# Attention heads of a streaming encoder: sample steps moved into the next head, a third gate tile, bf16 masks, cached values loaded at another place

## The chip, the cores and the metric

The kernel runs on one core of one Trainium2 chip. The metric is the time of one execution on the device in microseconds (us), as the median over runs. TensorE is called PE, its weight load PEld; VectorE is DVE, ScalarE ACT, GpSimd POOL. SP is the engine that issues most DMA transfers, in a queue that is worked off in order.

## The reference

One step of an encoder with two layers: a recurrent layer, then a stick-breaking attention layer with 16 heads of 128. There is one prompt of 512 frames and there are 8 samples of 16 frames, each with 512 cached frames of keys and values. Cut to the attention:

```
def sb_block(q, q_pos, k, v):
    z = einsum('bqhd,bshd->bhqs', q, k) * (HEAD_DIM ** -0.5)
    mask = arange(k.shape[1])[None, :] < q_pos[:, None]
    log_keep = where(mask, log_sigmoid(-z), 0.0)
    log_after = cumsum(log_keep, axis=3, reverse=True) - log_keep
    attn = where(mask, exp(log_sigmoid(z) + log_after), 0.0)
    return einsum('bhqs,bshd->bqhd', attn, v)

def stick_breaking_mixer(hn, k_all, v_all, w_in, w_out):
    q, zg = split(hn @ w_in, 2, axis=-1)
    o = stick_breaking(q.reshape(B, T, N_HEADS, HEAD_DIM), k_all, v_all)
    return (o.reshape(B, T, D_ATT) * silu(zg)) @ w_out
```

The rest of the layer (norms, modulation, residual) and the recurrent layer lie outside the change.

## The kernel before

All 640 frames (512 of the prompt, 128 of the samples) stay on the chip in columns, split into a high and a low part, and each product is three matmuls (high by high, low by high, high by low: the lines L108, L109 and L110 of a helper). The attention layer is done head by head, in `heads`. While head h is attended to, TensorE also works out the query and the gate of head h+1, by a scheme of block products with fewer multiplications. These are 180 matmuls of 320 columns a head, into banks named `psh`; they are cut into 8 pieces, one for each `q` in the order below (a generator that is asked for its next piece). The gate of a head lies in the tile `z`, and the attention's result is multiplied into it.

The steps of one head, by the letters of the order:

- P, the prompt's scores: 9 matmuls of `kh` and `ql`, `kl` and so on into three banks z3, z2, z1 (L1702 to L1704), and the scores against the samples' new keys `kn` (L1809). Behind each bank `sticks` follows, on ACT: Abs, Exp, Ln (L1637, L1638, L1639); on DVE: max and add (L1642), the scan with `keep` (L1645), a subtraction (L1648); on ACT the closing exponential (L1649); and on POOL the multiply by `mask` (L1653).
- S0, S1, the samples' scores against the cached keys `ck`, four samples each, into `zc` (L1727), with sticks of their own.
- V0, V1, the turns of the prompt's weights: transposes into `pa` (L1713), 7 in V0 and 3 in V1, evacuated by ACT into `ath` and by DVE into `atl` (L1720).
- T0, T1, the turns of the samples' weights: four transposes into `pas` (L1751), which ACT evacuates to `at`, and one into `pan` (L1755), which DVE evacuates to `an`. At its start T issues the loads of two tiles of cached values `cv` (512 KB each, two slots in all).
- M0, M1, the samples' sums `pos`: 4 matmuls with the new values `vn` (L1763), 16 with `cv` (L1768), then ACT evacuates to `ob` (L1771).
- C0, C1, the close: a transpose of `ob` into `pot` (L1775), which DVE multiplies into the gate `z` (L1778). C1 also splits the finished head (`oh` on ACT, L1790, and the rest on DVE, L1791) and writes both to DRAM from POOL's queue.
- O, the prompt's sum `po` (12 matmuls), multiplied into the gate by DVE.
- L and U load the next head's keys and values, K and W split them, N loads the next head's first cached keys.

The last head has an order of its own, in which `q` is a piece of the output product with `w_out_b` (`acc`), and Z the last gates; behind its scores the queue of SP loads the finished heads back (`yh`, `yl`, 20 transfers) and then the output's weights (`wr`).

The two lines that set the order are

```
    LAST = "P S0 q q q S1 V0 q V1 q Z T0 M0 O q C0 q T1 q M1 q C1 q"
    ORDER = "P q q S0 L q q V0 V1 S1 T0 O U q M0 q T1 N K q C0 M1 W q C1"
```

A scheduler then orders the instructions of each engine by readiness and priority; splits of weights (L1367, L1368, L1379) and evacuations of query products (L1530, L1535) have a raised priority.

Of the kernel before, what the change touches and what calls it, by code (L numbers as in the profile page):

```python
# [11 lines left out]
F32 = mybir.dt.float32  # L12
# [38 lines left out]
class Trunk:  # L51
# [1238 lines left out]
    def attention_consts(self, ap):  # L1290


        G = self.nc.gpsimd
        self.mask = [ap.tile([P, n], F32, name=f"mask{i}") for i, n in enumerate((P, TS))]
        self.keep = [ap.tile([P, n], F32, name=f"keep{i}") for i, n in enumerate((PAST, PAST + TS))]
        for v in self.mask + self.keep:
            G.memset(v, 1.0)

        def before(v, base):

            G.affine_select(v, v, pattern=[[-1, v.shape[1]]], compare_op=ALU.is_gt, fill=0.0, base=-base, channel_multiplier=1)

        before(self.mask[0], 0)
        before(self.keep[0], 1 - (PAST - P))
        for j in range(4):
            r = slice(32 * j, 32 * j + 32)
            before(self.mask[1][r, :], 0)
            before(self.keep[1][r, :], 1 - PAST)
# [155 lines left out]
    def query_tiles(self, ap):  # L1464
# [3 lines left out]
        z = ap.tile([P, T], F32, tag="z", name="z", bufs=2)  # L1468
# [219 lines left out]
    def attention(self, h, ap, qkv, zs):  # L1688
# [56 lines left out]

        def sample_turn(g):
            e = st[f"es{g}"]
            st["cv"] = [cached_values(4 * g + 2 * u) for u in range(2)]
# [10 lines left out]
        def sample_out(g):  # L1759
# [4 lines left out]
            if g == 0:  # L1764
                st["vn"] = new_values(1)
            for i in range(4):
                for j in range(4):
                    mm(po[32 * j : 32 * j + 32, 0:P], at[:, i, 32 * j : 32 * j + 32], cvs[j // 2][:, 4 * (j % 2) + i, :],  # L1768
                       start=False, stop=i == 3, **kw)
            ob = st["ob"] = ap.tile([P, P], F32, tag="ob", name="ob", bufs=1)  # L1770
# [61 lines left out]
        st = {"vn": new_values(0)}  # L1832
        steps = {"P": prompt_scores, "O": prompt_out}
# [10 lines left out]
    LAST = "P S0 q q q S1 V0 q V1 q Z T0 M0 O q C0 q T1 q M1 q C1 q"  # L1844
    ORDER = "P q q S0 L q q V0 V1 S1 T0 O U q M0 q T1 N K q C0 M1 W q C1"

    def heads(self, count=NHEAD):
        with self.pool("att") as ap:
# [9 lines left out]
            k, v = self.keys_split(ap, keys), self.values_split(ap, values)  # L1858
            for h in range(count):
# [4 lines left out]
                for step in (self.ORDER if more else self.LAST).split():  # L1864
# [5 lines left out]
                    elif step in steps:  # L1870
                        steps[step]()
                    elif more and step == "L":
# [7 lines left out]
                    elif more:  # L1880
                        v = self.values_split(ap, values)
        return out
# [136 lines left out]
```

## Time and profile before

| | us |
|---|---|
| median of 3 runs | 2858.66 |
| lowest, highest | 2856.97, 2867.83 |
| profiled execution: span | 2852.1 |
| profiled execution: its own total | not listed |
| heads 0 to 15 in the span | 2005.92 to 2648.68 |
| head 0 | 45.95 |
| heads 1 to 14, together | 550.77 |
| head 15 | 46.04 |

The span runs from the first to the last instruction of the profiled execution; the runs' times hold what lies around it as well, so the median stands 6.6 above the span. A head is counted from its first score matmul (L1702, 512 columns) to that of the next; head 15 runs to the end of the stage. In the rows quoted below, a wait row names the waiting engine, tile and line, what ended the wait, the sum of the waits in us, their count and the longest; a timeline row has the start in us, the duration in us, engine, line, operation, out<-in, tile sizes and count, and in brackets the idle time before it.

### The profile page before, as it was taken

The numbers are of one execution on the slowest core, as the hardware profiler recorded it, in microseconds if no ns is written. First come the engines' busy times: TensorE is split into PE (matmuls) and PEld (weight loads), VectorE is DVE, ScalarE is ACT, GpSimd is POOL, SyncE is SP. The second block draws the span as 40 slices with busy tenths as digits, with TensorE's granted clock in tenths as the row PEclk, the third lists the DMA queues.
The fourth block names the chain that finished last, engine by engine and source line by source line (L and its number), as shares of the span: only waits on it lengthen the run. The fifth ranks groups of instructions, "written<-read, shape, count | busy, mean of one in ns | idle before, by whom it ended". The sixth has DMA issues, their size and how long they took to land.

```text
span 2852.1 us, 48054 instructions
## 1 busy us (share of the span) xinstructions
PE 2785.0 (98%) x18340; PEld 2459.3 (86%) x18340; DVE 2034.8 (71%) x3344; ACT 1666.2 (58%) x2846; POOL 439.1 (15%) x732
## 2 busy tenths in 40 slices
PE   6999999999999999999999999999999999999998
PEld 4799999999999987777787899867888889887887
DVE  7678777777777766766866866667877877776335
ACT  5576556655665556665655555553666766666223
POOL 0012212221222111112220000122101111111000
PEclk9999999999999999999999999999999999999999
DMA  9966766676766666676776233575466666668636
GB/s 339 331 145 157 166 161 153 158 164 160 161 149 164 141 228 209 206 251 190 238 255 218 92 117 109 183 267 192 145 205 189 194 197 191 199 199 287 188 111 229
DMA packets 249094, 544.49 MB, mean 191 GB/s; under 512 B 23496, under 2 KB 108616, under 8 KB 247712
## 3 DMA queue, kind: packets, MB, share of 16 engines
q1 hardware_dynamic: 201616, 377.05, 41.2%
q0 software_dynamic: 47248, 164.38, 23.2%
q8 instruction: 144, 2.36, 0.3%
q14 instruction: 86, 0.70, 0.1%
HBM read 499.97 MB, written 41.37 MB: 190 GB/s over the span
## 4 chain that ended last, share of the span: by engine, by line
PE 80%; DVE 4%; ACT 4%; DMA 3%; issue 2%; POOL 0%; SPq 0%; DVEq 0%; POOLq 0%; ACTq 0%
PE acc L108 7%; PE acc L110 7%; PE acc L109 7%; PE pa L108 4%; PE pa L110 4%; PE pa L109 4%; PE psh L108 3%; PE psh L110 3%; PE psh L109 3%; PE pc L110 3%; PE pc L109 3%; PE pc L108 3%; PE acck L108 3%; PE acck L109 2%; PE acck L110 2%
## 5 line engine op out<-in xcount | busy, mean ns | idle before, releaser
L108 PE MATMUL acc<-wh,yh 128*128 128x512 f32 x940 | 371.0, 395 | 0.5 <-ACT wh L93 0.4
L110 PE MATMUL acc<-wh,yl 128*128 128x512 f32 x940 | 365.5, 390 | 1.3 <-DVE yl L962 1.3
L109 PE MATMUL acc<-wl,yh 128*128 128x512 f32 x940 | 366.4, 390 | 0.1
L94 DVE TENSOR_TENSOR wl<-wr,wh 128x1024 fp32r<-128x1024 f32 x151 | 186.5, 1238 | 217.0 <-ACT wh L93 216.6
L93 ACT ACTIVATE wh<-wr 128x1024 fp32r<-128x1024 f32 x151 | 159.6, 1057 | 267.7 <-PE acc L110 220.7
L108 PEld LDWEIGHTS acc<-wh,yh 128*128 128x128 f32 x940 | 176.7, 188 | 54.0 <-issue 15.7
L110 PEld LDWEIGHTS acc<-wh,yl 128*128 128x128 f32 x940 | 176.3, 188 | 38.8 <-DVE yl L962 1.7
L109 PEld LDWEIGHTS acc<-wl,yh 128*128 128x128 f32 x940 | 176.5, 188 | 36.3 <-DVE wl L94 0.7
L193 DVE TENSOR_TENSOR wa<-wa 128x1024 f32<-128x1024 f32 (+1 forms) x160 | 191.5, 1247 | 11.8 <-ACT wa L192 11.2
L110 PE MATMUL pa<-xs,wl 128*128 128x320 f32 x630 | 194.8, 309 | 0.5 <-DVE wl L94 0.5
L108 PE MATMUL pa<-xs,wh 128*128 128x320 f32 x630 | 194.7, 309 | 0.0
L109 PE MATMUL pa<-xs,wh 128*128 128x320 f32 x630 | 194.7, 309 | 0.0
L93 ACT ACTIVATE wh<-sum 128x896 fp32r<-128x896 f32 x102 | 96.9, 950 | 143.0 <-PE pa L109 46.5
L192 ACT ACTIVATE wa<-wa 128x1024 bf16<-128x1024 f32 x160 | 159.3, 1046 | 25.5 <-DVE wa L193 12.0
L546 POOL DMA_DIRECT2D sum<-w_in_a_dram x90 | 79.1, 882 | 490.5 <-DVE wl L94 208.8
L108 PE MATMUL psh<-nh,wl 128*128 128x320 f32 x480 | 150.8, 314 | 2.1 <-DVE z L1535 2.1
L110 PE MATMUL psh<-nh,wl 128*128 128x320 f32 x480 | 150.1, 313 | 0.0
L109 PE MATMUL psh<-nl,wl 128*128 128x320 f32 x480 | 149.4, 311 | 0.0
L93 ACT ACTIVATE wh<-rv 128x256 fp32r<-128x256 f32 (+1 forms) x108 | 51.8, 480 | 145.8 <-PE pa L109 95.2
L108 PE MATMUL acck<-wh,nh 128*128 128x512 f32 x320 | 127.8, 401 | 5.7 <-DVE keep L1263 3.5
L110 PE MATMUL pc<-xs,wl 128*128 128x320 f32 x420 | 129.9, 309 | 0.7 <-DVE wl L94 0.7
L108 PE MATMUL pc<-xs,wh 128*128 128x320 f32 x420 | 130.0, 310 | 0.0
(489 smaller groups left out, 8595.9 us busy)
## 6 DMA issues: line engine op xcount, KB each, us to landing
wa<-w_ada_dram POOLq DMA_DIRECT2D x120, 512.0 KB, 5.2
wr<-w_out_a_dram SPq DMA_DIRECT2D x96, 512.0 KB, 4.5
sum<-w_in_a_dram POOLq DMA_DIRECT2D x90, 448.0 KB, 5.7
wa<-w_ada_dram SPq DMA_DIRECT2D x72, 512.0 KB, 6.4
wr<-w_in_b_dram SPq DMA_DIRECT2D x64, 512.0 KB, 4.3
ck<-cache_k_dram SPq DMA_DIRECT2D x64, 512.0 KB, 5.2
cv<-cache_v_dram SPq DMA_DIRECT2D x64, 512.0 KB, 5.7
wr<-w_out_b_dram SPq DMA_DIRECT2D x55, 512.0 KB, 4.2
```

Source lines behind the costliest of these rows:

```text
L93: self.split_at = nc.scalar.activation(hi[:, :n], raw, AF.Copy).ins
L94: nc.vector.tensor_tensor(lo[:, :n], raw, hi[:, :n].bitcast(F32), ALU.subtract)
L108: mm(out, sh, mh, start=start, stop=False, **kw)
L109: mm(out, sh, ml, start=False, stop=False, **kw)
L110: return mm(out, sl, mh, start=False, stop=stop, **kw)
L192: nc.scalar.activation(parts[i], raw, AF.Copy)
L193: nc.vector.tensor_tensor(parts[2] if i else raw, raw, parts[i], ALU.subtract)
L546: self.nc.gpsimd.dma_start(self.big[tag], self.quarter(w, i), accum_op=ALU.add)
```

## The change

M1 and C1 of a head are left out of its own order and run inside the next head, as `m1` and `c1`: the second sum behind the prompt's scores, the close after one piece of query products. X stands behind m1 and loads the new values and the first two tiles of cached values; the second two are issued behind M0's matmuls, so that each load stands right behind the last sum that uses its slots. The turns V0, V1 and T0 are set apart by pieces of products, T0 stands ahead of S1, M0 ahead of O. The last head's order takes m1, X and c1 in the same way. The gate `z` gets a third tile, since the gate of the head before is now in use longer; masks and keeps are bf16, which takes 2368 bytes a partition less (the third z takes 2560).

```diff
@@ -1291,8 +1291,8 @@
 
 
         G = self.nc.gpsimd
-        self.mask = [ap.tile([P, n], F32, name=f"mask{i}") for i, n in enumerate((P, TS))]
-        self.keep = [ap.tile([P, n], F32, name=f"keep{i}") for i, n in enumerate((PAST, PAST + TS))]
+        self.mask = [ap.tile([P, n], BF16, name=f"mask{i}") for i, n in enumerate((P, TS))]
+        self.keep = [ap.tile([P, n], BF16, name=f"keep{i}") for i, n in enumerate((PAST, PAST + TS))]
         for v in self.mask + self.keep:
             G.memset(v, 1.0)
 
@@ -1465,7 +1465,7 @@
         qh = ap.tile([P, TP], F32R, tag="qh", name="qh", bufs=1)
         ql = ap.tile([P, TP], F32R, tag="ql", name="ql", bufs=1)
         qs = ap.tile([P, P + TS], F32, tag="qs", name="qs", bufs=1)
-        z = ap.tile([P, T], F32, tag="z", name="z", bufs=2)
+        z = ap.tile([P, T], F32, tag="z", name="z", bufs=3)
         self.q = (qh, ql, qs, z)
         return self.q
 
@@ -1743,9 +1743,12 @@
             dma(c, I["cache_v"][b0 : b0 + 2, :, h, :].rearrange("b (i p) d -> p (b i) d", p=P))
             return c
 
+        def values_begin(g):
+            st["vn"] = new_values(g)
+            st["cv"] = [cached_values(4 * g + 2 * u) for u in range(2)]
+
         def sample_turn(g):
             e = st[f"es{g}"]
-            st["cv"] = [cached_values(4 * g + 2 * u) for u in range(2)]
             ps = one("pas")
             for i in range(4):
                 tr(ps[:, P * i : P * i + P], e[:, P * i : P * i + P], self.ident)
@@ -1761,12 +1764,12 @@
             po = one("pos")
             for j in range(4):
                 mm(po[32 * j : 32 * j + 32, 0:P], an[:, 32 * j : 32 * j + 32], st["vn"][:, j, :], start=True, stop=False, **kw)
-            if g == 0:
-                st["vn"] = new_values(1)
             for i in range(4):
                 for j in range(4):
                     mm(po[32 * j : 32 * j + 32, 0:P], at[:, i, 32 * j : 32 * j + 32], cvs[j // 2][:, 4 * (j % 2) + i, :],
                        start=False, stop=i == 3, **kw)
+            if g == 0:
+                values_begin(1)
             ob = st["ob"] = ap.tile([P, P], F32, tag="ob", name="ob", bufs=1)
             A.activation(ob, po[:, 0:P], AF.Copy)
 
@@ -1829,8 +1832,8 @@
         o = zs
         if h == NHEAD - 1:
             o = self.outs.tile([P, 2, 3 * HALF], F32R, tag="ks1", name="o", bufs=1)[:, 0, :T].bitcast(F32)
-        st = {"vn": new_values(0)}
-        steps = {"P": prompt_scores, "O": prompt_out}
+        st = {}
+        steps = {"P": prompt_scores, "O": prompt_out, "X": lambda: values_begin(0)}
         for g in range(2):
             steps[f"V{g}"] = lambda g=g: prompt_turn(g)
             steps[f"T{g}"] = lambda g=g: sample_turn(g)
@@ -1841,8 +1844,8 @@
 
 
     STAY = (NHEAD - 2,)
-    LAST = "P S0 q q q S1 V0 q V1 q Z T0 M0 O q C0 q T1 q M1 q C1 q"
-    ORDER = "P q q S0 L q q V0 V1 S1 T0 O U q M0 q T1 N K q C0 M1 W q C1"
+    LAST = "P m1 X S0 q c1 q q S1 V0 q V1 q Z T0 M0 O q C0 q T1 q M1 q C1 q"
+    ORDER = "P m1 X q c1 q S0 L q V0 q V1 T0 q S1 M0 N O U q C0 K q W T1 q"
 
     def heads(self, count=NHEAD):
         with self.pool("att") as ap:
@@ -1856,6 +1859,7 @@
             keys, values = self.keys_load(0, ap), self.values_load(0, ap)
             self.ck = self.cached_keys(0, 0, ap)
             k, v = self.keys_split(ap, keys), self.values_split(ap, values)
+            before = {}
             for h in range(count):
                 qh, ql, qs, zs = self.q
                 steps = self.attention(h, ap, (qh, ql, qs, *k, *v), zs)
@@ -1869,6 +1873,8 @@
                             self.silu(ap, zs, j)
                     elif step in steps:
                         steps[step]()
+                    elif step in ("m1", "c1"):
+                        before.get(step.upper(), lambda: None)()
                     elif more and step == "L":
                         keys = self.keys_load(h + 1, ap)
                     elif more and step == "U":
@@ -1879,6 +1885,7 @@
                         k = self.keys_split(ap, keys)
                     elif more:
                         v = self.values_split(ap, values)
+                before = steps
         return out
```

On TensorE, where one head ends and the next begins (head 6; `pot` is a close, `pos` a sum, `z` with a number a bank of scores, of which only the first and the last are shown). Before:

```order
L1775 MATMUL pot<-ident,ob 128x128
L1763 MATMUL pos<-vn,an 32x128 x4
L1768 MATMUL pos<-cv,at 32x128 x16
L108 MATMUL psh<-nh,wh 128x320
...
L1775 MATMUL pot<-ident,ob 128x128
L1702 MATMUL z_23239<-kh,qh 128x512
...
L1809 MATMUL z_23270<-kn,qs 32x16 x8
L108 MATMUL psh<-nh,wh 128x320
```

After:

```order
L1702 MATMUL z_23206<-kh,qh 128x512
...
L1812 MATMUL z_23237<-kn,qs 32x16 x8
L1766 MATMUL pos<-vn,an 32x128 x4
L1769 MATMUL pos<-cv,at 32x128 x16
L108 MATMUL psh<-nh,wh 128x320
...
L1778 MATMUL pot<-ident,ob 128x128
L108 MATMUL psh<-nh,wl 128x320
```

Before, the second sum stood between the close C0 and 12 products, and C1 ended the head. Now it stands behind the scores, 27 products lie between it and its close, and 33 behind that; a head ends with 12 products behind the turn T1.

On TensorE in the middle of the same head, the turns and the sums. Before:

```order
L1713 MATMUL pa<-ident,e 128x128 x7
L1727 MATMUL zc<-ck,qs 32x512 x4
...
L1713 MATMUL pa<-ident,e 128x128
...
L1713 MATMUL pa<-ident,e 128x128 x2
...
L1751 MATMUL pas<-ident,e 128x128 x4
...
L1755 MATMUL pan<-ident,e 16x128
L109 MATMUL psh<-nl,wl 128x320
L108 MATMUL po<-ath,vh 128x512
...
L1763 MATMUL pos<-vn,an 32x128 x4
L1768 MATMUL pos<-cv,at 32x128 x16
```

After:

```order
L1713 MATMUL pa<-ident,e 128x128 x7
...
L1713 MATMUL pa<-ident,e 128x128 x3
...
L1754 MATMUL pas<-ident,e 128x128 x4
L1758 MATMUL pan<-ident,e 16x128
...
L1727 MATMUL zc<-ck,qs 32x512 x4
L1766 MATMUL pos<-vn,an 32x128 x4
L1769 MATMUL pos<-cv,at 32x128 x16
L108 MATMUL po<-ath,vh 128x512
```

Before, S1 and three gaps of 5 products, then one of 4 and one of 1, lay between the turns and the prompt's sum. Now 24 products lie between V0 and V1, 10 between V1 and T0, `pan` stands directly behind `pas`, and S1 and M0 stand behind T0 and 2 products, ahead of the prompt's sum.

On ACT behind the start of a head, after the change (`ez` belongs to the gate, `e` to the sticks; z_23206 is z3, z_23219 z2, z_23237 z1):

```order
L1637 ACTIVATE e<-z_23206 128x512
L1458 ACTIVATE ez<-ez 128x320
L1638 ACTIVATE e<-e 128x512
...
L1638 ACTIVATE e<-e 128x256
L1530 ACTIVATE qr<-psh 128x320
L1367 ACTIVATE wh<-wr 128x512
L1649 ACTIVATE e<-e 128x512
L1639 ACTIVATE e<-e 128x256
L1774 ACTIVATE ob<-pos 128x128
```

Before, `ob` of the second sum stood ahead of all of these, in the head it belonged to:

```order
L1448 ACTIVATE qs<-qr 128x128
L1771 ACTIVATE ob<-pos 128x128
L1367 ACTIVATE wh<-wr 128x512
L1457 ACTIVATE ez<-z 128x320
L1790 ACTIVATE oh<-z 128x640
```

The evacuation of the second sum moved behind the closing exponential of z3, and one weight split (L1367) stands between the first Abs and that exponential where there were two.

On SP's queue in the last head. Before:

```order
L949 DMA yh<-odh 128x640
L1743 DMA cv<-cache_v_dram 128x8x128 x2
L103 DMA wr<-w_out_b_dram 128x1024 x3
L1743 DMA cv<-cache_v_dram 128x8x128 x2
L103 DMA wr<-w_out_b_dram 128x1024 x7
```

After, from the head's start:

```order
L949 DMA yh<-odh 128x640
L1738 DMA vn<-out_v_dram 16x4x128
L1743 DMA cv<-cache_v_dram 128x8x128 x2
L1684 DMA ck<-cache_k_dram 128x2x512 x2
L949 DMA yl<-odl 128x640
...
L1743 DMA cv<-cache_v_dram 128x8x128 x2
L103 DMA wr<-w_out_b_dram 128x1024 x7
```

The first two tiles moved ahead of the transfers of finished heads; the second two moved from behind three pieces of `w_out_b` to ahead of all of them.

## The prediction

> **What bounds the kernel now.** I read the page's first part, then the stage the change touches cut into windows, then PE's waits there, then the timeline of one head.
>
> ```profile
> span 2852.1 us, 48054 instructions
> PE 2785.0 (98%) x18340; PEld 2459.3 (86%) x18340; DVE 2034.8 (71%) x3344; ACT 1666.2 (58%) x2846; POOL 439.1 (15%) x732
> ...
> 2005.92:2051.87 45.95, 41.67 (x320) 35.24 (x318) 41.38 (x82) 33.41 (x78) 4.51 (x8) 1.00 0.48 146
> 2051.87:2602.64 550.77, 545.99 (x4755) 487.68 (x4754) 424.56 (x800) 372.47 (x829) 67.05 (x140) 1.00 0.64 197
> 2602.64:2648.68 46.04, 39.81 (x266) 29.49 (x265) 26.75 (x44) 25.89 (x48) 4.55 (x7) 0.93 0.95 330
> ...
> 2631.00:2637.00 6.00, 4.43 (x41) 3.11 (x37) 1.46 (x3) 2.28 (x3) 0.00 (x0) 0.52 0.89 317
> ```
>
> The window rows (stretch, length, busy PE, PEld, DVE, ACT, POOL, granted clock, DMA share, GB/s) are head 0, heads 1 to 14, head 15, and a piece of head 15. A head runs from its first prompt score to the next head's. TensorE is the bound: in heads 1 to 14, 39.34 us each, it is busy for 99%. [...]
>
> ```profile
> PE pa L1713 <- DVE atl L1720: 3.0, 4, 0.9
> PEld pan L1755 <- issue: 4.2, 12, 0.5
> PEld po L108 <- ACT at L1753: 2.3, 12, 0.2
> PE psh L108 <- DVE z L1535: 2.1, 1, 2.1
> PE zc L1727 <- issue: 1.0, 1, 1.0
> PE pos L1763 <- DMA vn<-out_v_dram: 0.5, 1, 0.5
> PE pos L1768 <- DMA cv<-cache_v_dram: 5.2, 2, 4.0
> ```
>
> These are waits (who, for whom: sum, count, longest): three rows of heads 1 to 14, three of head 0, one of head 15. No wait in the middle heads is large; the large one is the last head's, for cached values.
>
> Starts and durations of single matmuls, head 6 and, for the last four rows, head 13:
>
> ```profile
> 2250.16 0.48 PE L1702 MATMUL z<-kh,qh 128*128 128x512 f32 x1
> 2252.48 0.41 PE L108 MATMUL psh<-nh,wh 128*128 128x320 f32 x1
> ...
> 2269.61 0.93 PE L1713 MATMUL pa<-ident,e 128*128 128x128 f32 x7
> 2270.46 1.06 PE L1727 MATMUL zc<-ck,qs 128*32 128x512 f32 x8
> 2271.46 0.42 PE L108 MATMUL psh<-ks,wh 128*128 128x320 f32 x1
> 2271.71 0.31 PE L109 MATMUL psh<-ks,wh 128*128 128x320 f32 x1
> ...
> 2275.10 0.30 PE L108 MATMUL psh<-nh,wl 128*128 128x320 f32 x1
> 2275.55 0.27 PE L1755 MATMUL pan<-ident,e 128*16 128x128 f32 x1
> 2275.57 0.39 PE L109 MATMUL psh<-nl,wl 128*128 128x320 f32 x1
> 2275.94 0.50 PE L108 MATMUL po<-ath,vh 128*128 128x512 f32 x1
> 2276.27 0.40 PE L109 MATMUL po<-atl,vh 128*128 128x512 f32 x1
> 2276.51 0.39 PE L110 MATMUL po<-ath,vl 128*128 128x512 f32 x1
> 2276.74 0.33 PE L108 MATMUL po<-ath,vh 128*128 128x384 f32 x1
> ...
> 2560.05 0.27 PE L1775 MATMUL pot<-ident,ob 128*128 128x128 f32 x1
> 2560.25 0.42 PE L1763 MATMUL pos<-vn,an 16*32 16x128 f32 x8
> 2560.60 1.08 PE L1768 MATMUL pos<-cv,at 128*32 128x128 f32 x32
> 2561.61 0.42 PE L108 MATMUL psh<-nh,wh 128*128 128x320 f32 x1
> ```
>
> And a stretch of head 6 in which TensorE does nothing but query products (psh; length, PE busy, clock, DMA):
>
> ```profile
> 2253.00:2261.30 8.30, 8.30 (x59) 1.00 0.42 139
> ```
>
> Each lasts 0.4, so two or three of the 59 began before the stretch: they start 0.147 us apart. Prompt sums of 512 columns (po) settle at 0.23 (2276.51 to 2276.74). Beside that, starts at a change of kind show its price: 0.25 from the first psh after scores to the second, 0.20 from pot to pos, only 0.02 from a transpose to psh.
>
> **The change part by part.** The matmuls stay the same in number and shape; what moves is which stand next to which.
>
> *Waits that go, heads 1 to 14.* Before, the second prompt turn V1 follows V0 at once and waits for the evacuation of its bank: 3.0 us in four waits, from the row. Now 24 products (3.5 us) lie between: 0. The transpose pan stood behind one psh and started 0.45 after it, against 0.147 in a run: 0.30. Now it follows the pas transposes directly, and T0 stands ahead of S1 and the sum: 0.30 x 14 = 4.2, which is also the wait row's sum. Before, po followed one psh and waited a little on ACT: 0.37 to its start and 0.33 to the second product against 0.23, 0.14 + 0.10 = 0.24, x 14 = 3.4. Now M0 stands between. Together -10.6.
>
> *Switching.* A head now has 9 stretches of psh where it had 10. One less saves its entry and slow first product, (0.23 - 0.147) + (0.25 - 0.147) = 0.19. The old pot to pos step (0.20) becomes pot to psh (0.02): -0.18. The old pa to zc step, also about 0.2 (the last of 7 transposes starts near 2270.27, zc at 2270.46), becomes pa to psh: -0.17. Against this stand z to pos and pos to po, which no row shows; bounds are 0 (0.02, transpose to psh) and 0.20 (pot to pos); I take 0.1 each, the middle, since neither row is nearer. And zc to pos: by the row of zc to psh it is no dearer than before. Sum -0.54 + 0.2 = -0.34 a head, x 14 = -4.8. Ends: 0 (both steps full, the pa step not gained) and -7.6 (both free).
>
> *Waits that come.* Placing the second sum behind the prompt's scores puts its evacuation `ob` on ACT's queue behind the closing exponential of the prompt's first sticks, and C1's transpose waits for `ob`. Here is what ACT does there before:
>
> ```profile
> 2252.28 0.58 ACT L1637 ACTIVATE e<-z 128x512 f32<-128x512 f32 x1
> 2252.76 0.46 ACT L1459 ACTIVATE ez<-ez 128x320 f32<-128x320 f32 x1
> 2253.12 0.62 ACT L1638 ACTIVATE e<-e 128x512 f32<-128x512 f32 x1
> ...
> 2258.37 0.64 ACT L1649 ACTIVATE e<-e 128x512 f32<-128x512 f32 x1 [0.27 <-DVE e L1648]
> ```
>
> PE reaches C1's transpose at 2.32 (scores, 2250.16 to 2252.48) + 1.36 (M1: 0.35 for vn, 1.01 for cv) + 27 x 0.147 + 0.1 = 7.8 us after the head's start. On ACT the order lists 16 steps from the first Abs to `ob`: eight of 512 columns at 0.5, four of 320 at 0.36 (both by the starts above), three of 256 at about 0.27, `ob` 0.2: 6.45. The Abs stood 2.12 into the head, behind the gate's copy `oh` (640 columns, about 0.6), which now stands behind `ob`, so I put it at 1.4: `ob` ready at 7.85. That is even with PE's 7.8, so I take 0.1 a head, and 0.1 more for the first sample sum M0, which follows T0's evacuation `at` by S1 (1.0 us) alone. Sum +0.2 x 14 = +2.8. Ends: 0, if both are in time; +21, if the closing exponential stays at 8.2 as before: then `ob` is ready 0.5 + 0.3 + 0.3 later, at 9.3, 1.5 behind PE, x 14. I stay near the lower end because before two weight splits of 512 columns (L1367) stood between the first Abs and that exponential and one does now, and on DVE one of two such operations between the scan and L1648 went too. Queued behind the waiting transpose is all of PE.
>
> *Head 0.* No M1 and C1 stand at its end, 1.36 + 0.3 less; each head passes them on, and they come back in head 15, where PE waits for DMA in any case. The vn wait (0.5) goes, as vn is loaded at its head's start. The scores' second part stands earlier, with the key split put ahead on DVE, which takes most of the 1.0 of the zc wait, while the 2.1 for DVE at L1535 stays. Sum -3; ends -6 (that too, and the next evacuations follow) and 0 (the split delays the others).
>
> *Last head.* Before, SP put both loads of cached values for M0 behind 20 transfers of gated rows (yl, yh):
>
> ```profile
> 2622.77 1.96 SPq L1743 DMA_DIRECT2D cv<-cache_v_dram  x2
> ...
> 2630.73 0.64 PE L1768 MATMUL pos<-cv,at 128*32 128x128 f32 x4 [4.04 <-DMA cv<-cache_v_dram]
> ...
> 2633.76 1.06 ACT L93 ACTIVATE wh<-wr 128x1024 fp32r<-128x1024 f32 x1 [7.27 <-DMA wr<-w_out_b_dram]
> 2634.06 1.01 SPq L1743 DMA_DIRECT2D cv<-cache_v_dram  x2
> ```
>
> Now M0's values go ahead of them, and the wait of 5.2 and the slow matmuls behind it (clock 0.52 in 2631 to 2637: 4.43 busy, so about 2.1 over full speed) go: -7.3. What is late next is the same queue. The DMA engines are busy for 0.95 of this head (330 GB/s), and ACT waits 7.27 us for the first piece of w_out_b, so the output's products can't start before 2633.8 however early M0 is. This piece now stands behind 1 MB more, 3.2 us at 330 GB/s, since M1's values (two of 512 KB) keep the place M0's had. M1 also waits for those. PE has only prompt sums and two small sums to do meanwhile. So I take 0: the wait changes its name. Ends: -7.3 (all of it gained) and +3.2.
>
> On that slow clock, the Trainium skill's page "TensorE: Matmul & The Clock Gate", section "Part 1: The HAM clock gate (the "warmup" mystery)", states that the clock is halved after an idle window of about 3.4 us. The granted 0.52 right behind a wait of 4.04 us agrees. By it, a last head that waits in pieces shorter than that would keep its full clock, which is the 2.1 us in the -7.3 end; by my term of 0, it waits once more as long and loses it again.
>
> *No cost.* Masks in bf16 and the third z tile: the multiplies by mask run on POOL, which is busy for 67.05 of 550.77 us, and PE's wait at pa is on DVE's, not POOL's work; the scans that read keep run on DVE (424.56 of 550.77 us), over the same number of elements, so a slower scan would find slack. The third z tile takes away a reuse that has no row in PE's waits: 0. Of the loads issued behind the last sum that uses their two slots, the cached values have the longest way:
>
> ```profile
> cv<-cache_v_dram SPq DMA_DIRECT2D x64, 512.0 KB, 5.7
> ```
>
> They are needed 10 us after issue or later by the order (over 60 products and the turns between), which covers 5.7. With that cover gone each of 28 sums could wait up to 5.7.
>
> *Sum.* -10.6 - 4.8 + 2.8 - 3 + 0 = -15.6: span 2852.1 to 2836.5. The profiled execution's own total is not shown; the median of the runs, 2858.66, is 6.6 above the span, and 2836.5 + 6.6 = 2843.1. A change counts as one from about 0.5% (14.3 us: below 2844.4 or above 2873.0), so this forecast lies just past it.
>
> **The rivals.**
> - *New small waits eat half the gain.* Everything removed is 0.2 to 0.3 us a piece, and a wait of 0.4 a head at `ob`, M0 or the pas bank costs 5.6. For it: `ob` and PE are even in my count, ACT was late by 0.27 at the very exponential. Against it: PE's waits before are small throughout. 2843.1 + 8 (0.4 and a little more in 14 heads, and at head 0) = about 2851.
> - *C1 waits for `ob`* (slower). The closing exponential stays at 8.2: +21 instead of +2.8 gives -15.6 + 18.2 = +2.6, 2861.3; with the switching at its poor end 2866. It turns the change into a loss from 1.3 us of wait a head (18.4/14), and slower by 0.5% from 2.3 ((18.4 + 14.3)/14). For it: DVE was the releaser of that exponential and keeps most of its load. Against it: fewer steps stand ahead on both engines.
> - *The last head's wait really vanishes.* If the flood and w_out_b have slack that I don't see: -15.6 - 7.3 = -22.9, 2835.8. Against it: the 7.27 us wait of ACT on the same queue.
> - *The order does nothing*: PE's 99% means that what it saves at one boundary it loses at the next. Only if the 0.30 at pan and the 0.24 at po are PE's draining, and are paid at pas or S1 instead: then only the switching, head 0 and the pa wait stay, 2848 to 2856.
>
> **How the numbers follow.** The forecast (2838 to 2848) gets 0.50, small new waits 0.25, the vanishing last wait 0.10, no effect 0.05, waiting for `ob` 0.10. Faster by over 0.5% are the forecast's part under 2844.4, about 0.35, the last-head case 0.10, and 0.04 of the small waits, where they hit less than I set: 0.49. Slower by over 0.5% are the `ob` case from 2.3 us a head, 0.04, and sums that wait for their values in every head as well, 0.03: 0.07. Within: 0.44. The range goes from 2829.9 (the last-head case with switching at its better end and head 0 too: -22.9 - 2.8 - 3 = -28.7) to 2861 (the `ob` case as worked out); outside are a longer `ob` wait or waits for values, about 0.1, and some 0.05 below.
>
> **What would show it.** In the changed profile, heads 1 to 14 should take about 38.4 us each (39.34 - 12.6/14), head 15 again some 46, and the rows of pa, pan and po should be gone from PE's waits. A row of pot waiting on ACT `ob` of 0.5 us or more a head means the `ob` rival; pos waiting on DMA cv in the middle heads, that the loads moved too late. In the last head I expect pos to wait for cv still, now M1's, or acc for wh. I am wrong if PE's starts around pan and po keep 0.3 gaps elsewhere, or if the last head gets shorter by over 4 us.

## The result and the profile after

The changed kernel is slower: 2885.68 us median (2882.40 to 2889.36, 5 runs) against 2860.08 for the kernel before (2856.97 to 2867.83, 5 runs). The ratio is 1.0090, with a 95% interval of 1.0079 to 1.0102. The forecast was 2843.1 with a range of 2829.9 to 2861.0, 15.6 us faster; the change costs 25.6 us. The profiled execution after the change has a time of 2885.68 us and a span of 2883.8, so what lies around the span is about 2 us. If that holds before as well, most of the 6.6 us between the median and the span there comes from a profiled execution that was faster than the median. The forecast, a difference added to that median, isn't touched by this.

The page's first lines after the change, and windows for head 0, heads 1 to 14, and head 15 to the end (columns as in the prediction):

```profile
span 2883.8 us, 48097 instructions
PE 2790.6 (97%) x18340; PEld 2459.7 (85%) x18340; DVE 2037.1 (71%) x3344; ACT 1664.9 (58%) x2846; POOL 443.0 (15%) x732
...
2008.95:2053.48 44.53, 39.83 (x306) 34.54 (x305) 40.67 (x80) 33.36 (x78) 4.19 (x8) 1.00 0.49 151
2053.48:2631.43 577.95, 546.63 (x4727) 484.54 (x4725) 426.61 (x803) 370.16 (x829) 69.89 (x140) 1.00 0.59 188
2631.43:2883.84 252.41, 236.78 (x1159) 191.29 (x1159) 111.89 (x147) 87.03 (x136) 12.51 (x21) 0.97 0.62 198
```

Heads 1 to 14 take 27.2 us more (577.95 against 550.77) with the same busy time of PE (546.6 against 546.0): practically all of it is waiting. Head 0 is 1.4 shorter, the part from head 15 on 3.0 longer (it was 249.41). Another 3.0 stand ahead of the heads, where the kernels do the same work and executions differ by as much (head 0 starts at 2005.92 before, at 2008.95 here, and at 2006.2 to 2015.8 in the runs below). So the two spans differ by 31.7 us, the medians by 25.6.

The waits of heads 1 to 14, after the change:

```profile
ACT vh L1315 <- DMA vr<-out_v_dram: 32.9, 11, 4.0
ACT wh L1364 <- DMA wr<-w_in_b_dram: 14.4, 13, 2.2
PE z L1702 <- ACT qh L1446: 13.9, 13, 2.0
ACT kh L1315 <- DMA kr<-out_kT_dram: 13.7, 11, 1.8
PE pas L1754 <- DVE atl L1720: 13.3, 11, 2.3
PEld pot L1778 <- ACT ob L1774: 3.9, 13, 0.3
PE pos L1766 <- DVE an L1760: 2.2, 2, 1.2
```

The three rows of ACT for a DMA stood before as follows (same view, kernel before):

```profile
ACT vh L1315 <- DMA vr<-out_v_dram: 10.7, 14, 2.6
ACT wh L1364 <- DMA wr<-w_in_b_dram: 5.0, 7, 1.3
ACT kh L1315 <- DMA kr<-out_kT_dram: 3.5, 6, 1.4
```

PE has two new waits, neither of them in the prediction: the scores of the next head wait for the query `qh`, and T0's transposes wait for V1's evacuation. In both cases the engine waited for was itself held up: ACT works its queue in order, and a split of loaded data (`vh`, `kh`, `wh`) stood in front, waiting for a DMA.

Why the loads are late is read in two more views. The issues of DMA, median us from issue to landing (the last column), first before, then after:

```profile
odl<-z POOLq DMA_DIRECT2D x14, 320.0 KB, 4.0
...
kr<-out_kT_dram SPq DMA_DIRECT2D x16, 256.0 KB, 2.6
vr<-out_v_dram SPq DMA_DIRECT2D x16, 256.0 KB, 2.8
```

```profile
odl<-z POOLq DMA_DIRECT2D x14, 320.0 KB, 6.7
...
kr<-out_kT_dram SPq DMA_DIRECT2D x16, 256.0 KB, 4.4
vr<-out_v_dram SPq DMA_DIRECT2D x16, 256.0 KB, 5.9
```

The same 256 KB of next values take twice as long. And head 6 after the change, pieces of 4 us from 8 us after its start on (last columns: clock, DMA share, GB/s); then, from the kernel before, the pieces 16 to 24 us and 28 to 32 us after its start:

```profile
2270.19:2274.19 4.00, 3.98 (x28) 3.84 (x28) 4.00 (x8) 1.59 (x4) 1.46 (x3) 1.00 0.28 71
2274.19:2278.19 4.00, 4.00 (x30) 2.97 (x29) 2.32 (x5) 3.14 (x7) 2.27 (x4) 1.00 0.16 53
2278.19:2282.19 4.00, 4.00 (x31) 4.00 (x31) 3.62 (x6) 2.26 (x5) 0.00 (x0) 1.00 0.99 308
2282.19:2286.19 4.00, 4.00 (x29) 3.84 (x27) 2.71 (x8) 2.69 (x8) 0.21 (x1) 1.00 1.02 400
...
2290.19:2294.19 4.00, 4.00 (x40) 3.68 (x29) 3.05 (x6) 3.34 (x9) 0.29 (x1) 1.00 0.90 258
2294.19:2298.19 4.00, 4.00 (x30) 3.99 (x29) 3.46 (x8) 1.23 (x3) 0.22 (x1) 1.00 1.10 324
```

```profile
2266.16:2270.16 4.00, 4.00 (x31) 3.99 (x30) 3.53 (x7) 2.00 (x5) 0.18 (x1) 1.00 0.91 325
2270.16:2274.16 4.00, 4.00 (x30) 2.82 (x29) 3.46 (x7) 3.62 (x10) 0.15 (x2) 1.00 0.66 196
2278.16:2282.16 4.00, 4.00 (x60) 3.60 (x53) 2.71 (x6) 1.91 (x4) 0.80 (x2) 1.00 0.55 145
```

The transfers of a head are the same as before, but they come in two bunches: the DMA engines are nearly idle from 8 to 16 us, and full from 16 to 24 and again, nearly or quite, from 28 to 36. The timeline of head 6 (starts at 2262.19) names what lies in them. First bunch, on POOL's and SP's queues and ACT:

```profile
2276.33 0.57 POOL L1796 DMA_DIRECT2D odh<-oh  x1 [0.41 <-ACT e L1637]
...
2276.54 0.89 SPq L1684 DMA_DIRECT2D ck<-cache_k_dram  x2
2279.77 0.34 SPq L1661 DMA_DIRECT2D kr<-out_kT_dram  x1
2280.20 4.75 SPq L1355 DMA_DIRECT2D wr<-w_in_b_dram  x3
...
2284.90 0.63 ACT L1315 ACTIVATE kh<-kr 128x512 fp32r<-128x512 f32 x1 [1.03 <-DMA kr<-out_kT_dram]
2285.97 0.53 ACT L1719 ACTIVATE ath<-pa 128x128 fp32r<-128x128 f32 x2
...
2287.12 0.66 PE L1754 MATMUL pas<-ident,e 128*128 128x128 f32 x4 [0.82 <-DVE atl L1720]
```

`kr` is loaded into the slot of the finished head `oh` (both have the tag "oh"), so it waits until `oh` is stored. With C1 in the next head that store is issued 14.2 us into it instead of 2.2, `kr` at 17.8 instead of 6.4 (means over heads 2 to 13), and three pieces of weights queue behind `kr` on SP. ACT then waits for `kr` with V1's evacuation behind, and PE for that.

Second bunch:

```profile
2290.57 1.36 SPq L1743 DMA_DIRECT2D cv<-cache_v_dram  x2
2291.98 1.84 SPq L1684 DMA_DIRECT2D ck<-cache_k_dram  x1
2293.93 0.41 SPq L1669 DMA_DIRECT2D vr<-out_v_dram  x1
...
2299.84 0.63 ACT L1315 ACTIVATE vh<-vr 128x512 fp32r<-128x512 f32 x1 [2.31 <-PE psh L110]
2301.41 0.58 ACT L1756 ACTIVATE at<-pas 128x512 f32<-128x512 f32 x1
2302.23 0.36 ACT L1446 ACTIVATE qh<-qr 128x192 fp32r<-128x192 f32 x1 [0.24 <-DVE qr L1535]
...
2302.64 0.50 PE L1702 MATMUL z<-kh,qh 128*128 128x512 f32 x1 [0.55 <-ACT qh L1446]
```

`vr` shares its slot with `ath`, which the prompt's sum O frees; O now stands behind S1 and M0 and ends 2.4 us later. And the cached values, issued right behind M0, stand ahead of `vr`, where before they stood behind it. `vr` lands 38.0 us into a head instead of 30.9 (mean over heads 2 to 13). `vh` holds ACT, then come two splits of weights, `at` and `qh`, and the next head's scores wait. (The row of `vh` names PE as releaser, which had long been done; `vr` landed at 2299.75.)

### The profile page after: what moved, and what is told of

Same layout as the page of the kernel before. It is cut to its first block, busy times and chain, and to the rows that moved or that the text cites. A ratio compares the mean times of both kernels' runs of the same rounds, so it can differ in the third digit from the quotient of the medians.

```text
span 2883.8 us, 48097 instructions
## 1 busy us (share of the span) xinstructions
PE 2790.6 (97%) x18340; PEld 2459.7 (85%) x18340; DVE 2037.1 (71%) x3344; ACT 1664.9 (58%) x2846; POOL 443.0 (15%) x732
## 4 chain that ended last, share of the span: by engine, by line
PE 76%; DMA 6%; DVE 5%; ACT 2%; issue 2%; SPq 1%; POOL 0%; DVEq 0%; POOLq 0%; ACTq 0%
PE acc L108 7%; PE acc L110 7%; PE acc L109 7%; PE pa L108 4%; PE pa L110 4%; PE pa L109 4%; PE pc L110 3%; PE pc L108 3%; PE pc L109 3%; DMA vr<-out_v_dram 3%; PE acck L108 2%; PE acck L109 2%; PE acck L110 2%; PE psh L108 2%; PE psh L110 2%; DMA wr<-w_in_b_dram 2%
```

## The experiments

Four theories are named in the expectations. Theory 1: late loads, through ACT's queue. Theory 2: the new neighbours on TensorE cost more than the old. Theory 3: bf16 operands are slower. Theory 4: ACT's queue is full, and what is taken out of the way makes room for another wait. Each experiment has its label in brackets, by which the expectations and the table further down name it. Ratios are against the kernel before on the same chip, intervals 95%. The experiments ran on several chips, on which the kernel before took 2855.8 to 2860.1 us, so they are compared with each other by ratio. The times of heads 1 to 14 are from one profile each (before 550.8, changed 578.0).

**Masks and third tile alone** (bf16_z3, on the kernel before):

```diff
-        self.mask = [ap.tile([P, n], F32, ...
-        self.keep = [ap.tile([P, n], F32, ...
+        self.mask = [ap.tile([P, n], BF16, ...
+        self.keep = [ap.tile([P, n], BF16, ...
...
-        z = ap.tile([P, T], F32, tag="z", name="z", bufs=2)
+        z = ap.tile([P, T], F32, tag="z", name="z", bufs=3)
```

> The kernel before with only the bf16 masks and the third gate tile, order unchanged. Theories 1 and 2: no effect, 2855 to 2866 us. Theory 3, by which a multiply or scan with a bf16 operand is slower and holds up the sticks: over 2870.

Measured: ratio 1.0003 (0.9992 to 1.0014), heads 1 to 14 550.7. No effect; theory 3 falls.

**Values from POOL's queue** (vr_pool):

```diff
-        self.nc.sync.dma_start(raw, self.O["v"]...
+        self.nc.gpsimd.dma_start(raw, self.O["v"]...
```

> The changed kernel, with the load of the next head's values (vr) issued from POOL's queue instead of SP's. Theory 1 (late loads): in the changed kernel vr stands on SP behind two tiles of cached values and one of cached keys, lands 5.8 us after its issue, and ACT's split of it (vh) waits 32.9 us over heads 1 to 14, with the weights' evacuation at and the query qh queued behind; the next head's scores then wait 13.9 on PE. With vr on a queue of its own ACT's wait for it falls below 10 and PE's wait at the scores below 5: 2868 to 2877 us. Theory 2 (TensorE's new neighbours: scores behind products, sum behind scores, cost more than the old ones): no change, 2882 to 2890.

Measured: ratio 1.0172 (1.0148 to 1.0196), slower still, and outside both theories' ranges. Wait and landing:

```profile
ACT vh L1315 <- DMA vr<-out_v_dram: 36.7, 13, 6.0
...
vr<-out_v_dram POOLq DMA_DIRECT2D x16, 256.0 KB, 6.3
```

SP's queue is not what makes `vr` late: from another queue it takes 6.3 us as well, with the same bytes ahead of it on the DMA engines. The Trainium skill's page "DMA: Bandwidth & Descriptors", section "Issuing engines are not separate DMA queues", states that all issuing engines use the same 16 DMA engines. The trace agrees, 6.3 us against 5.9. (A cost of POOL's queue by itself isn't separated: `vn`, 32 KB, takes 3.8 us from it and 2.0 from SP in the changed kernel, though at other moments of the head.) ACT's order also changed: `vh` came ahead of the first `qh`, and PE waited at `pan` (19.5 us in 14 waits) instead of the scores.

**Keys in another slot** (kr_at; `at` instead of `oh`):

```diff
-        raw = ap.tile([P, T], F32R, tag="oh", name="kr", bufs=1).bitcast(F32)[:, :TP]
+        raw = ap.tile([P, 4, P], F32, tag="at", name="kr", bufs=1).rearrange("p a n -> p (a n)")
...
-    ORDER = "P m1 X q c1 q S0 L q V0 q V1 T0 q S1 M0 N O U q C0 K q W T1 q"
+    ORDER = "P m1 X q c1 q S0 L q V0 K q V1 T0 q S1 M0 N O U q C0 q W T1 q"
```

> The changed kernel, with the next head's keys (kr) loaded into the slot of the samples' evacuated weights (at) instead of that of the finished head (oh), and their split K moved ahead of V1 so that the slot is free for T0. Theory 1: since C1 now runs in the next head, oh is stored only 17.5 us into it, kr waits for that slot, three pieces of weights queue behind kr on SP, and ACT's splits of both hold up the evacuation of V1, for which T0's transposes wait 13.3 us on PE over 14 heads. With the slot free early kr is issued some 10 us earlier, PE's wait at pas goes below 3, ACT's wait for w_in_b from 14.4 below 5: 2869 to 2877 us; the wait for vr stays. Theory 2: 2882 to 2890.

Measured: ratio 1.0143 (1.0120 to 1.0165), slower; a miss.

```profile
ACT wh L1364 <- DMA wr<-w_in_b_dram: 18.8, 13, 2.6
...
PE pas L1754 <- DVE atl L1720: 9.0, 9, 1.8
```

`kr` did come early (issued at 5.4), but V1's evacuation now stood behind the next split that waits for a DMA, `wh` of L1364. Taking one late load out of the way exposed the other. S1 was also torn apart on PE (the scores of one sample ahead of T0, of three behind), which the changed kernel doesn't have.

**Keys loaded one step later** (l_late):

```diff
-    ORDER = "P m1 X q c1 q S0 L q V0 q V1 ...
+    ORDER = "P m1 X q c1 q S0 q V0 L q V1 ...
```

> The changed kernel, with the load of the next head's keys one step later (L behind V0), by which three pieces of weights no longer queue behind kr on SP while kr waits for the store of oh, and ACT's split of kr stands behind the evacuation of V1. Theory 1: V1's evacuation ends about 1 us earlier, the wait at pas (0.87 a head) goes to below 0.2: 2870 to 2878 us, with the wait for vr as it was. Theory 4: the split of kr, now late, holds up T0's evacuation at, and M0 waits: 2883 or more.

Measured: ratio 1.0148 (1.0132 to 1.0165), a miss of the same kind, in theory 4's range but not by its path (it had `at` and M0 wait): `kr` landed at 25.0 us, `wh` of L1364 kept ACT waiting 19.1 us ahead of V1's evacuation, and S1 was torn apart as well.

**Sum and close back in their own head** (own_end; the last head's order likewise):

```diff
-    ORDER = "P m1 X q c1 q S0 L q V0 q V1 T0 q S1 M0 N O U q C0 K q W T1 q"
+    ORDER = "P X q q S0 L q V0 q V1 T0 q S1 M0 N O U q C0 K q W T1 M1 q C1"
```

> The changed kernel, with M1 and C1 back at the end of their own head (order P X q q S0 L q V0 q V1 T0 q S1 M0 N O U q C0 K q W T1 M1 q C1); turns stay spread apart, cached values are loaded behind the last sum. Theory 1: oh is stored early again, so the wait at pas goes, but vr stands where it stood, and M1 directly behind T1 waits for at as well: 2866 to 2878 us. Theory 2, by which the carry into the next head is what costs: back to 2855 to 2862.

Measured: ratio 1.0142 (1.0118 to 1.0165). Theory 2 would have brought it back to the kernel before; it isn't, and theory 1's range is missed as well. The keys are early again (2.6 us to landing), `vr` is not (6.4), M1 right behind T1 waits 24.3 us for `an`, and S1 is torn apart here too. This tells little of the carry itself, since that wait is of my own making.

**Values in the slot of `oh`, from POOL, ahead of O** (vr_ohp):

```diff
-        raw = ap.tile([P, 3, 512], F32R, tag="ath", name="vr", ...
-        self.nc.sync.dma_start(raw, self.O["v"]...
+        raw = ap.tile([P, T], F32R, tag="oh", name="vr", ...
+        self.nc.gpsimd.dma_start(raw, self.O["v"]...
...
+    ORDER = "P m1 X q c1 q S0 L q V0 q V1 T0 q K U S1 M0 N O q C0 q W T1 q"
```

> The changed kernel, with the next head's values vr loaded into the slot of oh and kr (free once kr is split, 24 us into the head) instead of that of ath (free only when the prompt's sum has ended, 30.4), from POOL's queue; K is put ahead of it. Theory 1, narrowed by the first runs: vr is late because its slot comes free 2.4 us later than before (O stands behind S1 and M0) and because 2 MB of cached keys and values are put on the DMA engines right ahead of it, so that it takes 6.2 us instead of 2.9 on any queue; ACT's split vh waits for it with at and qh behind. Loaded 6 us earlier, ACT's wait for vr goes to about 0, the step from the last product to the next head's scores from 1.31 to 0.4 us or less, 14 heads: 2868 to 2876 us; the wait at pas stays at 0.9 a head. Theory 4 (ACT's queue is full there, something else takes the place of vh): 2880 or more.

Measured: ratio 1.0063 (1.0048 to 1.0078), 2873.56 us, as theory 1 had it. `vr` is issued at 23.9 and lands at 28.8; ACT's wait for it and PE's wait at the scores have no rows any more. The wait at pas grew from 13.3 to 18.4.

**Prompt's sum ahead of M0, T0 a piece later** (o_t0):

```diff
+    ORDER = "P m1 X q c1 q S0 L q V0 q V1 q T0 S1 O U M0 N q C0 K q W T1 q"
```

> The changed kernel, with T0 behind one more piece of products and the prompt's sum O back ahead of M0 (V1 q T0 S1 O U M0). Theory 1: the wait at pas is for the evacuation of V1 (ends 25.1 us into the head), with M0 tied to it through at and an; with 12 products between V1 and T0 and with O between T0 and M0 both waits go (0.87 and 0.12 a head, 13.9 us), and O ends 1 us earlier, ahead of the cached values, so vr lands earlier and ACT's wait for it falls by half (another 5 to 8): 2862 to 2872 us. Theory 4: the evacuation moves later with the turn, 2880 or more.

Measured: ratio 1.0028 (1.0014 to 1.0042), 2863.82 us, in theory 1's range, though not by its parts. Now `vr` stands ahead of the cached values on SP and takes 3.9 us; the scores don't wait, which is more than was expected. The wait at pas, which was to go, went only from 13.3 to 11.3 us.

**Both of these** (vr_o_t0):

```diff
+    ORDER = "P m1 X q c1 q S0 L q V0 q V1 q T0 K U S1 O M0 N q C0 q W T1 q"
```

> The edits of vr_ohp and o_t0 together. Theory 1: all the new waits go, about 2.3 us a head: 2849 to 2860 us, no slower than the kernel before. Theory 4: 2875 or more.

Measured: ratio 1.0052 (1.0036 to 1.0069), 2870.40 us, a miss: no better than either of the two. With `vr` cured twice over, what is left is the wait at pas, 18.7 us in 14 heads, and ACT's wait for `kr`, 24.2: the first bunch.

**Only the cached values back at their old place** (cv_t1):

```diff
         def values_begin(g):
             st["vn"] = new_values(g)
-            st["cv"] = [cached_values(4 * g + 2 * u) for u in range(2)]
+            if g == 0:
+                st["cv"] = [cached_values(2 * u) for u in range(2)]
...
         def sample_turn(g):
             e = st[f"es{g}"]
+            if g == 1:
+                st["cv"] = [cached_values(4 + 2 * u) for u in range(2)]
```

> The changed kernel with only the second two tiles of cached values loaded where they were before (at the start of T1; SP then holds one of them ahead of vr and one behind), order of the steps unchanged. Theory 1: one tile and one of cached keys less stand ahead of vr on the DMA engines, so vr lands 1 to 2 us earlier, the next head's scores wait 0.5 to 1 us less a head: 2871 to 2880 us. If the late slot of vr alone sets its landing: no change, 2882 to 2889.

Measured: ratio 1.0031 (1.0019 to 1.0043), 2865.42 us, below both ranges, less than even theory 1 asked for. Heads 1 to 14 and the wait:

```profile
2054.38:2616.26 561.88, 545.70 (x4727) 487.05 (x4726) 427.52 (x803) 370.00 (x829) 69.93 (x140) 0.99 0.62 193
...
ACT vh L1315 <- DMA vr<-out_v_dram: 22.0, 12, 3.6
```

So putting the two tiles back, alone, takes away 0.59 of the 0.90% (1.0090 to 1.0031). `vr` lands only some 2 us earlier (35.9), but that is nearly enough for `qh` to be in time: the step from the last product to the scores falls from 1.31 to 0.27 us (table below).

**Turns repaired: V1 next to V0, keys in the slot of `at`, O ahead of M0** (o_v01_kr):

```diff
-        raw = ap.tile([P, T], F32R, tag="oh", name="kr", ...
+        raw = ap.tile([P, 4, P], F32, tag="at", name="kr", ...
...
+    ORDER = "P m1 X q c1 q S0 L q V0 V1 K q T0 q S1 O U M0 N q C0 q W T1 q"
```

> The changed kernel with O ahead of M0 as in o_t0, V1 directly behind V0 again (one piece of products between V1 and T0), and the keys kr in the slot of at as in kr_at. What is left in o_t0 is a wait at pas (0.64 a head over its free value) for the evacuation of V1, which stands on ACT behind splits that wait for a DMA (of kr; in kr_at, of w_in_b). In this order no split of data on the way stands ahead of V1's evacuation. Theory 1: the wait at pas goes to below 0.2, pa waits about 0.1 a head for its bank: some 38.8 us a head against 39.43 of o_t0, 2850 to 2860 us. Theory 4 (something else takes its place on ACT): 2862 or more.

Measured: ratio 0.9984 (0.9973 to 0.9995), 2852.82 us, in theory 1's range: faster than the changed kernel, and by 0.16%, little beyond the interval, than the kernel before.

```profile
2052.08:2599.84 547.76, 541.39 (x4724) 486.38 (x4720) 429.47 (x801) 371.05 (x829) 71.20 (x140) 1.00 0.64 199
```

ACT still waits for `vr` (24.3) and for w_in_b (24.9), but nothing that PE needs soon stands behind.

**Only the close carried over** (hyb), and **neither carried, turns spread** (own_q2; the last head's order likewise in both):

```diff
+    ORDER = "P c1 X q q S0 L q V0 q V1 q T0 S1 O U M0 N q C0 K q T1 q M1 W"
...
+    ORDER = "P X q q S0 L q V0 q V1 q T0 S1 O U M0 q N T1 K q C0 M1 W q C1"
```

> Only the close C1 is carried into the next head (directly behind its scores), the sum M1 stays at its own head's end behind one piece of products; T0 one piece later and O ahead of M0 as in o_t0 (order P c1 X q q S0 L q V0 q V1 q T0 S1 O U M0 N q C0 K q T1 q M1 W). Theory 1: oh is stored some 8 us earlier than in the changed kernel, so kr, the weights behind it and the store no longer fall together with the cached keys between 14 and 22 us of a head; the waits at pas and at the scores go; M1 may wait 0.3 to 0.5 for at and an: 2848 to 2858 us. Theory 2 (the carry of the sum is what brings the gain at the neighbours): 2860 or more.

> M1 and C1 back in their own head with the tail of the kernel before (q T1 K q C0 M1 W q C1), the turns spread, O ahead of M0: order P X q q S0 L q V0 q V1 q T0 S1 O U M0 q N T1 K q C0 M1 W q C1. Theory 1: with the store of oh early again kr and the weights come early, vr stands ahead of the cached values on SP, so neither the scores nor pas wait; T1 may wait about 1 us for the sticks of S1, which is 4 us later than in the kernel before: 2850 to 2866 us. Theory 4 (spreading the turns itself is what costs, through ACT): 2870 or more.

Measured: 1.0053 (1.0032 to 1.0074) and 1.0085 (1.0066 to 1.0105), both misses for theory 1, on the side of its rivals (theory 2 in the first, theory 4 in the second). Loads are early in both, as expected (`vr` 3.8 and 3.7 us), and the scores don't wait. But the scheduler put the scores of one sample of S1 ahead of T0 and those of three behind in both, which by the starts costs 0.86 of the 1.46 us a head that the first takes over o_v01_kr (steps from and between `zc`: 2.96 against 2.10). In the second T1 waits for the sticks of S1 (9.6 us in 10 waits). So neither run settles its rival, and what the carry is worth by itself stays open.

**The turns repaired without O, without and with the old place of the cached values** (v01_kr and cv_v01_kr; both have the keys in the slot of `at` as above, the second has the edit of cv_t1 as well):

```diff
+    ORDER = "P m1 X q c1 q S0 L q V0 V1 K q T0 q S1 M0 N O U q C0 q W T1 q"
```

> The changed kernel with only the repair of the turns: V1 directly behind V0, keys kr in the slot of at and split ahead of T0; O and the cached values stay where the change put them, so vr stays late. Theory 1: the wait at pas goes (0.87 a head, 12 us), the wait at the scores (1.3 a head) stays: 2871 to 2880 us. If the two waits hide each other (whoever is rid of one waits longer at the other): 2881 or more.

> The same with the second two tiles of cached values loaded at the start of T1 as before (v01_kr and cv_t1 together); O still behind M0. Theory 1: both waits go, 0.8 a head less than cv_t1: 2852 to 2859 us. If O ahead of M0 is needed as well: 2861 or more.

Measured: 1.0079 (1.0063 to 1.0095) and 1.0031 (1.0021 to 1.0040): the first is not clear of the changed kernel's 1.0090, the second is no faster than cv_t1 alone, so O ahead of M0 is needed as well, the second branch of its expectation. The wait at pas is gone in both, and stands at M0 instead (first of the two):

```profile
PEld pos L1766 <- ACT z L1530: 20.1, 13, 2.4
...
PE z L1702 <- ACT qh L1446: 9.6, 12, 1.5
```

T0's evacuation `at` is now what stands behind the late `wh` (the row names `z`, the evacuation next to it on ACT), and M0 follows T0 by 12 products and S1. O between S1 and M0, 2.1 us of work, covers it in o_v01_kr.

**The last head's cached values at their old place** (best2, on o_v01_kr):

```diff
+            if g == 0 or h < NHEAD - 1:
+                st["cv"] = [cached_values(4 * g + 2 * u) for u in range(2)]
...
+            if g == 1 and h == NHEAD - 1:
+                st["cv"] = [cached_values(4 + 2 * u) for u in range(2)]
```

> o_v01_kr, the fastest so far, with the last head's second two tiles of cached values issued at the start of its T1, as in the kernel before, so that the first pieces of w_out_b stand ahead of them. In the changed kernel the part from head 15 on takes 3.0 us longer than before (252.4 against 249.4), in cv_t1 only 1.2. Theory 1: 1 to 2.5 us less than o_v01_kr, 2849 to 2853 us; if the end is set by M1's own products carried into it: no change.

Measured: ratio 0.9985 (0.9977 to 0.9994), 2852.12 us. The part from head 15 on fell from 252.5 to 251.1 in the profile; in the times that can't be told from o_v01_kr.

## Why the prediction was wrong

The steps on PE, in us a head, worked out from the starts of matmuls in heads 2 to 13 (from one start to the next, summed over the steps of a kind):

| step | before | changed | cv_t1 | o_t0 | v01_kr | o_v01_kr |
|---|---|---|---|---|---|---|
| last product to scores | - | 1.31 | 0.27 | 0.15 | 1.03 | 0.15 |
| within the scores | 2.21 | 2.43 | 2.28 | 2.12 | 2.40 | 2.12 |
| product to pas, two | 0.30 | 1.17 | 1.07 | 0.94 | 0.30 | 0.29 |
| S1 to the sum behind it | - | 0.64 | 0.69 | 0.72 | 1.28 | 0.63 |
| to and within pa | 1.51 | 1.17 | 1.17 | 1.17 | 1.71 | 1.71 |
| to pan, two | 0.53 | 0.22 | 0.22 | 0.22 | 0.22 | 0.22 |
| product to po | 0.35 | - | - | - | - | - |
| product to pot, two | 0.30 | 0.50 | 0.49 | 0.49 | 0.49 | 0.49 |
| whole head | 39.29 | 40.92 | 39.67 | 39.43 | 40.90 | 39.12 |

- *Waits that go*: right in mechanism, and in size within a third. pa, pan and po fell by 0.34, 0.31 and 0.35, together 1.00 x 14 = 14.0 us against 10.6 (po's whole step went, of which I had counted 0.24). *Switching* gave nothing, +0.06 a head against -0.34 (so the new neighbours hardly cost anything either, which speaks against theory 2): the steps that I priced came out near what I set (z to pos 0.11, pot to psh 0.05) or at their bound (pos to po 0.20), but I left out that the scores now stand behind a product (0.15) instead of a transpose (0.03), and S0 and S1 both behind a product (0.48 for two) where one stood behind pa (0.43). The two terms together gave 13.2 us of the 15.4 forecast.
- *Waits that come*: this step failed. I set +2.8 us with ends of 0 and +21. Against the free values (0.15 at the scores, 0.30 at pas, 0.52 behind S1) the changed kernel waits 1.16 at the scores, 0.22 within them, 0.87 at pas, 0.12 at M0 and 0.20 at pot: 2.57 a head, 36 us (and 1.63 more a head in sum, which is 40.92 against 39.29). Head 1 lost 2.5 and head 14 lost 5.1 (44.25 against 39.14): there V1's evacuation stood behind a split of w_out_b as well, pas waited 2.26 us in one piece, and the granted clock was 0.50 from 2613.5 to 2616.9. I looked only at what the moved steps themselves wait for. `ob` for one was right: ready 8.1 us into the head against 7.85 worked out, and C1's transpose waits 0.1. Heads 1 to 14 took 41.3 us each instead of the 38.4 foreseen, and neither row that was to warn of it came: pot waited 0.28 us a head for `ob`, against a sign of 0.5, and pos never waited for cv in these heads. Both rows watch the moved steps only.
- *No cost*, the loads: the other half of the failure. I asked when the cached values are needed, found 10 us, and set 0. That was true of their own reader; but I didn't ask what they are put in front of. `vr`, next on the same DMA engines, has no such slack. cv_t1 shows this term alone at 0.59% (17 us); o_t0, in which `vr` gets ahead of the cached values because O comes earlier, has 0.62% (18 us). Also, "the third z tile takes away a reuse" looked at one slot; the slots of `oh` (shared with `kr`) and `ath` (shared with `vr`), which the moved C1 and O free later, were not looked at.
- *The rivals*: the slower one had the right place on ACT's queue and the wrong item in it. ACT's closing exponential was not late; the splits that wait for DMAs were.
- *Head 0*: -1.4 against -3, within its ends. *Last head*: +3.0 against 0, near its upper end; the wait for cv is 2.0 us instead of 5.2, and the end is set by the queue, as argued. cv_t1 and best2, with the second tiles behind the first pieces of w_out_b, get 1.5 to 1.8 of it back in one profile each, where two kernels with the same last head (before and bf16_z3, 249.4 and 250.4) differ by 1.0.
- How the 25 us divide depends on the order in which things are put back, because one wait hides another. Taken alone, the place of the cached values makes 17 of them (cv_t1), O ahead of M0 with T0 a piece later 18 (o_t0), both through the late `vr`; the repair of the turns alone makes 3, within the noise (v01_kr), and nothing on top of cv_t1 (cv_v01_kr), since the wait moves from pas to M0. On top of o_t0 the repair makes 13 (1.0028 against 0.9984). So the path over o_t0 adds up to the 30 us between the changed kernel and o_v01_kr, about 18 for the late `vr` and 13 for V1's evacuation behind late splits; the two are not terms that could be had one by one. That a wait which is taken away comes back elsewhere (kr_at, l_late, vr_ohp, v01_kr) is theory 4, so theories 1 and 4 are two halves of one account. Of the 15 us forecast, 4 to 5 are left in o_v01_kr against the kernel before; it has V1 next to V0 again, so the steps at pa are back (1.71), and what makes up the rest isn't separated.

## What to carry to other kernels

When a step is moved, price not its own wait but what its slots and its transfers are ahead of: list for each load that the step issues or frees which load stands behind it, and when that one's reader stands in line. An engine that works its queue in order, prepares data and also empties another engine's banks can pass a late load on to that engine. It does so only where an urgent evacuation stands behind the late split: in o_v01_kr ACT waits 24.3 us for `vr` and PE hardly at all, in the changed kernel ACT waits 32.9 us and PE 13.9. If a repair only moves the wait (pas to M0, `kr` to `wh`), find the whole chain, and put independent work between its last links.

## What the hardware showed

- The landing time of a load followed what else was in flight more than its queue: the 256 KB of `vr` took 2.8 us in the kernel before, at a DMA share of 0.55, and 5.9 us from SP or 6.3 from POOL behind 1.5 to 2 MB at a share near 1. From POOL, but issued 23.9 us into the head, they took 4.9 (vr_ohp).
- From the last matmul of a group of sample scores to the next start it is 0.52 us where nothing waits, whatever comes next (psh, po, pos or pas), so tearing a group into one and three pays that twice.
- The clock fell in the last head though no wait was long. Its windows of 1 us and its wait row, after the change (columns: PE busy, clock, DMA share, GB/s):

```profile
PE pos L1769 <- DMA cv<-cache_v_dram: 2.0, 2, 1.1
...
2661.00:2662.00 1.00, 0.35 (x4) 1.00 1.14 305
2662.00:2663.00 1.00, 0.70 (x5) 1.00 1.16 296
2663.00:2664.00 1.00, 0.42 (x8) 1.00 1.18 301
2664.00:2665.00 1.00, 0.41 (x4) 0.85 1.06 372
2665.00:2666.00 1.00, 0.05 (x4) 0.50 1.03 398
```

No wait exceeds 1.2 us, and yet the granted clock is 0.50 from 2665 on, after 4 us in which PE was busy for 1.88. So the sentence in the prediction by which waits in short pieces would keep the clock is refuted; what preceded the fall is the low share of the whole stretch. Head 14 shows the same with one wait: 2.26 us at pas, and the clock at 0.50 from 2613.5 on. That is how the Trainium skill's page "TensorE: Matmul & The Clock Gate", section "Part 1: The HAM clock gate (the "warmup" mystery)", describes the gate, by activity in a window; the trace agrees with that part of it.
